# Memory's matrices woven with the first gated units, and the last pair's sum on VectorE, in a hybrid encoder layer

## The chip, the cores and the metric

The kernel runs on one core of a Trainium2 chip. The metric is the device time of one execution in microseconds. The core has five engines that run side by side: TensorE (PE in the profile, with its weight loads as PEld), VectorE (DVE), ScalarE (ACT), GpSimd (POOL) and SyncE (SP), whose queue issues most DMA transfers; ScalarE's queue issues a few.

## The reference, cut to what matters

One layer of an encoder on 2048 tokens of width 1024, batch 1, all in float32:

```python
y = rmsnorm(h, norm_mix_g) @ w_in            # q, k, v (8 heads of 64), a and g (512 each)
att = dilated_sliding_attention(q, k, v)     # three patterns (window, dilation), joined by a softmax of their log-sums
conv = silu(layernorm(conv31(a * sigmoid(g)) + conv_b))
h = h + concat([att, conv]) @ w_out
xq = rmsnorm(h) @ w_xq
xk, xv = rmsnorm(mem) @ w_xk, rmsnorm(mem) @ w_xv      # mem: 256 rows
h = h + softmax(xq @ xk.T / 16) @ xv @ w_xo            # 4 heads of 256
h = h + square(relu(rmsnorm(h) @ w_up)) @ w_down       # 4096 wide
out = rmsnorm(h, norm_final_g)
```

Everything that depends on `mem` is known before any token is read, so the kernel multiplies it together once: w_xq with xk (the matrices "a", `ascr`) and xv with w_xo (the matrices "b", `bscr`). These are "memory's matrices". The three patterns of attention give three partial results with their minima and sums; a "pair" is two neighbouring heads, and "the pair's sum" joins its three partial results.

## The kernel before, in words

**Precision.** Each matmul operand is split in a high half (rounded to fp32r) and a low half (the rest). A product takes three matmuls, high by high, high by low, low by high (`mm3`, L197 to L200). A weight tile is loaded as `raw` (128 x 1024, 512 KB), its high half is a cast on ScalarE, its low half a subtraction on VectorE or POOL (`wsplit2`, L186; `split` in `memory`, L380).

**The planner.** The program is traced in an order written out by hand: generators that yield, and `weave` (L92), which takes one step of a main generator and then, by a rate, steps of the others; `run` (L455) does the same with whole numbers of steps. A scheduler then goes through the traced instructions by priority in the order of the trace, on a simulated time line, and gives each engine and each DMA queue its order: what stands earlier in the trace goes first, and what is ready in the simulation fills the gaps. `pinned` and `after` (L78 to L90) hold an instruction behind a given one on its engine. On the chip each engine and each queue keeps that order strictly. A tile waits until the last tile in its place (same pool and tag) has been read for the last time; PSUM tiles share eight banks by kind (`banks`, L65).

**First stage (L710 to L727).** Token group n (of four, 512 tokens each) has a room `x{n}` of eight tiles for its high and low halves of normalized x. `memory` (L346) makes memory's matrices: after two first steps eight steps for w_xk (`proj`), twelve for w_xq (`xq`, transposed; four heads, two tiles each), eight for w_xv, twelve for w_xo (four heads, two tiles each). It borrows the room of group 3 for its activations and, for its weights, two places in the weight pool and two in the room of group 2 (`wtiles`, L371): four raw tiles, four high and four low halves in turn. `xprep(n)` (L320) loads 512 rows of x, takes their norms and, in eight steps, transposes 128 columns of all four blocks on PE, copies the transpose out (`xts`, L334, to the scratch `xscr`), scales it (`xv`, L337) and splits it (L338 ScalarE, L339 POOL). The order is `run([memory, xprep 0 and 1], (3, 1))`, then the gated units `glu(0)` and `glu(1)` on groups 0 and 1 (`glu`, L490: g through a sigmoid, a times that), of which one step and then seven are woven with `xprep` 2 and 3 at a rate of 2.5. Then `edges` (L700) writes zero rows from a tile in a raw weight place, and `lin_qk` (L589) projects keys and queries with their rotary part (`ct`, `sn`, L634 to L645) on all four groups.

**Values and the first convolution (L737 to L747).** `lin_v` projects v; the depthwise convolution of group 0 (`conv0`, 31 steps of 128x512 on VectorE per channel block, L213 and L215) is woven into it, in the last part at a rate of 1.2.

**Attention on group 0 (L1080 to L1110).** The far pattern is done for all tokens here. The gated units on groups 2 and 3 (`rest`) run ahead for 32 steps and then at 0.8 of a step per step of attention; the layernorm of the convolution (`conv_ln`, L221) stands first in the weave. A unit of attention has scores (`s`), masked minimum and exponential (L762, L763), transposes (L769), probabilities in two halves (L772, L773) and products with v (L777 to L779).

**A pair's sum (`combine`, L871).** It loads two partial results (`ld`), takes the minimum on VectorE (L890, L891), and then, on engine `W`, which is POOL: differences (L892, L894), after an exponential on ScalarE (L898) the weighted sums (L900 to L905), after a reciprocal on VectorE (L909) the weights (L912) and the weighted parts (L916, L918). The result `cat` is transposed on PE (L926), split (`ct`, L928, L929), stored to the scratch `cath` and `catl`, and loaded again for the output projection by `load_cat` and `load_pair` (L1154 to L1170). For group 0, `load_pair` for the last two pairs is called late, inside `resid_linear` (L1172), ahead of the last third of the first three output tiles.

**After that (`post`, L1197)** come, for each group, the output projection, cross attention, and the wide layer, woven with the attention and the convolution of the next group; the first six steps of `post(0)` are woven with the end of attention on group 0.

Of the kernel before, what the change touches and what calls it, by code (L numbers as in the profile page):

```python
# [21 lines left out]
P = 128  # L22
S = 2048
D = 1024
H = 8
# [22 lines left out]
def hybrid_layer(ctx, tc, A, out):  # L48
# [16 lines left out]
    banks = {"mm": (0, 1, 2), "a": (3, 4), "b": (5, 6), "c": (7,), "mem": "b"}  # L65
# [254 lines left out]
    def xprep(sp, n):  # L320
# [8 lines left out]
        for k in range(KC):  # L329
            pt = ps("a", f"xt{n}_{k}")  # L330
            for j in range(4):
                PE.transpose(pt[:, j * P:(j + 1) * P], nat_cols(nat[j], k), ident)
# [4 lines left out]
            DVE.scalar_tensor_tensor(xv, pt, gain("mix", k), rbs, op0=ALU.mult, op1=ALU.mult)  # L337
            ACT.copy(XH_[k, n], xv)  # L338
            POOL.tensor_tensor(XL_[k, n], xv, f(XH_[k, n]), op=ALU.subtract)  # L339
            yield  # L340
# [5 lines left out]
    def memory(sp):  # L346
# [24 lines left out]
        def wtiles(name, shape=(P, 8, P)):  # L371
            i = cnt[0] % 4
            cnt[0] += 1
            if i < 2:
                return [wp.tile(list(shape), dt, tag=t, name=f"m{t}_{name}", bufs=2)
                        for t, dt in (("raw", F32), ("whi", F32R), ("wlo", F32R))]
            return [xpool(q, j, 2, f"m{q}{j}_{name}", shape, dt)
                    for q, j, dt in (("h", i - 2, F32), ("h", i, F32R), ("l", i, F32R))]

        def split(src, name, shape=(P, 8, P)):  # L380
            raw, hi, lo = wtiles(name, shape)
            dma(raw, src)
            ACT.copy(hi, raw)
            DVE.tensor_tensor(lo, raw, f(hi), op=ALU.subtract)
            return hi, lo

        def proj(w, name, th, tl):

            for j in range(KC):
                wh, wl = split(wcols(w, j * P), f"{name}{j}")  # L390
                pt = ps("mm", f"p{name}{j}")[:, 0:256]
# [13 lines left out]
        for h in range(XH):  # L405
# [15 lines left out]
            for k2 in range(4):  # L421
                pt = ps("mm", f"pa{h}{k2}")
# [12 lines left out]
        for h in range(XH):  # L435
# [4 lines left out]
            for mc in range(2):  # L440
                for nh in range(2):
                    pt = ps("mm", f"pb{h}{mc}{nh}")
# [11 lines left out]

    def run(gens, steps):  # L455

        live = list(zip(gens, steps))
        while live:
            for g in list(live):
                for _ in range(g[1]):  # L460
                    if next(g[0], live) is live:
                        live.remove(g)
                        break
# [246 lines left out]
    with ExitStack() as st:  # L710
# [26 lines left out]
    with ExitStack() as st:  # L737
# [8 lines left out]
        weave(steps, (conv0, 1.2))  # L746
# [123 lines left out]

    def combine(p, pr, o0):  # L871
# [15 lines left out]
        W = POOL  # L887
# [33 lines left out]
        ct = [aq.tile([P, 512], F32R, tag=f"ct{x}", name=f"ct{x}{p}{pr}") for x in "hl"]  # L921
# [8 lines left out]
        for t, d in zip(ct, (cath, catl)):  # L930
            dma(f(d[pr][:, 512 * p:512 * (p + 1)]), f(t))
# [150 lines left out]
    with ExitStack() as st:  # L1082
# [5 lines left out]
        for _ in range(32):  # L1088
# [63 lines left out]
    cats = {}  # L1152

    def load_cat(p, half):  # L1154
# [17 lines left out]
    def resid_linear(load, rhs, korder, resid, hs, ssum, key, y, name, late=None):  # L1172


        for ms in ((0, 1, 2), (3,), (4,), (5,), (6,), (7,)):
            wt = [load(m) for m in ms]
            pts = {}
            for i, ks in enumerate((korder[0:4], korder[4:6], korder[6:8]) if len(ms) > 1 else (korder,)):
                if late and len(ms) > 1 and i == 2:
                    late()  # L1180
                for m, (wh, wl) in zip(ms, wt):
# [4 lines left out]
                    if late and ks[-1] != korder[-1]:  # L1186
# [10 lines left out]
    def post(p):  # L1197
# [9 lines left out]
        def from_x(m):  # L1207
# [8 lines left out]
                                (lambda: load_pair(0, 1, 1)) if p == 0 else None)  # L1216
# [195 lines left out]
```

## Time and profile before

| | us |
|---|---|
| median of 3 runs | 2928.93 (2924.41 to 2935.4) |
| the profiled execution's own time | 2929.9 |
| its span, first to last instruction | 2928.1 |
| PE busy in it | 2845.6 |

The profile is of one execution. Busy time of an engine is the time covered by its instructions; a row of a group gives the line, engine, operation and tiles, the count, then busy us and mean ns of one, and the idle time ahead of them with what ended it. A row of the timeline gives the start in us from the span's start, the duration, the instruction, and in brackets how long its engine had been idle and what released it. A row of a stretch gives its length and each engine's busy time in it, the mean clock that TensorE was granted (1 is full speed) and the share of the DMA engines' time.

### The profile page before, as it was taken

To read this page: it belongs to the slowest core of one execution; us is meant where nothing else is said; L and a number is where in the kernel's file an instruction comes from. 1 tells how busy PE (TensorE), PEld (TensorE's weight loads), DVE (VectorE), ACT (ScalarE), POOL (GpSimd) and SP (SyncE) were. 2 spreads that over 40 slices of the span, in tenths; PEclk is the share of its full clock that TensorE was granted. 3 is DMA by queue.
4 is the path that set the end of the run, shared out by engine and by line. 5 is a ranking of instruction groups with operands and counts; after the bars stand their busy time and mean duration, and the time that the engine had idled before them with its cause. 6 is when DMAs were issued, how large, how long until landed. Compare 5 with 4: busy or idle time off the path is not lost.

```text
span 2928.1 us, 42935 instructions
## 1 busy us (share of the span) xinstructions
PE 2845.6 (97%) x16396; PEld 2426.2 (83%) x16396; DVE 1845.9 (63%) x3295; ACT 1186.9 (41%) x2002; POOL 462.9 (16%) x518
## 2 busy tenths in 40 slices
PE   8999999989799999999999999999999999999999
PEld 7878789878698888888888888888888888888887
DVE  5636544555568877566697865577877555544445
ACT  5632211566435333444443344344433443432233
POOL 1335421122101220210020122000210110000000
PEclk9999999999899999999999999999999999999999
DMA  8978854799724444455344445534444355333332
GB/s 263 304 161 205 194 146 135 172 239 230 206 93 133 129 134 136 138 167 172 97 128 129 136 130 177 181 101 131 121 132 132 113 153 173 94 93 94 96 99 73
DMA packets 620806, 434.89 MB, mean 149 GB/s; under 512 B 191333, under 2 KB 549785, under 8 KB 620600
## 3 DMA queue, kind: packets, MB, share of 16 engines
q1 hardware_dynamic: 582168, 414.05, 50.3%
q10 hardware_dynamic: 38432, 18.09, 2.6%
q8 instruction: 129, 2.11, 0.3%
q14 instruction: 77, 0.63, 0.1%
HBM read 340.42 MB, written 91.64 MB: 148 GB/s over the span
## 4 chain that ended last, share of the span: by engine, by line
PE 75%; DMA 4%; ACT 2%; DVE 2%; SPq 2%; issue 1%; POOL 1%; ACTq 0%; POOLq 0%; DVEq 0%
PE dn L198 8%; PE dn L199 8%; PE dn L200 8%; PE up L198 8%; PE up L200 8%; PE up L199 7%; PE xs L198 2%; PE xs L199 2%; PE xs L200 2%; PE o L198 2%; PE o L199 2%; SPq L57 2%; PE o L200 2%; PE pt L769 2%; PE s L979 2%; PE x L198 2%
## 5 line engine op out<-in xcount | busy, mean ns | idle before, releaser
L198 PE MATMUL up<-mh,whi_u 128*128 128x512 f32 x1024 | 402.9, 394 | 1.3 <-DVE rl L1283 1.1
L199 PE MATMUL dn<-hhl,whi_d 128*128 128x512 f32 (+1 forms) x1056 | 402.5, 385 | 0.4 <-DVE hhl L1286 0.4
L200 PE MATMUL dn<-hhh,wlo_d 128*128 128x512 f32 (+1 forms) x1056 | 401.6, 384 | 0.0
L198 PE MATMUL dn<-hhh,whi_d 128*128 128x512 f32 (+1 forms) x1056 | 400.3, 391 | 0.1
L200 PE MATMUL up<-mh,wlo_u 128*128 128x512 f32 x1024 | 399.4, 390 | 0.0
L199 PE MATMUL up<-ml,whi_u 128*128 128x512 f32 x1024 | 398.6, 389 | 0.0
L215 DVE SCALAR_TENSOR_TENSOR cacc<-cu,cw,cacc 128x512 f32<-128x512 f32 x480 | 387.7, 808 | 5.8
L189 ACT CAST whi_u<-raw_u 128x1024 fp32r<-128x1024 f32 x128 | 134.6, 1052 | 428.2 <-PE dn L199 358.5
L1301 DVE TENSOR_TENSOR h<-h,dn 128x512 f32<-128x512 f32 (+1 forms) x264 | 172.5, 668 | 203.3 <-PE dn L200 202.3
L189 ACT CAST whi_d<-raw_d 128x1024 fp32r<-128x1024 f32 x128 | 134.4, 1050 | 355.4 <-PE up L199 318.3
L200 PEld LDWEIGHTS dn<-hhh,wlo_d 128*128 128x128 f32 x1056 | 198.5, 188 | 39.3
L198 PEld LDWEIGHTS dn<-hhh,whi_d 128*128 128x128 f32 x1056 | 197.5, 188 | 39.3 <-DVE h L1301 3.5
L199 PEld LDWEIGHTS dn<-hhl,whi_d 128*128 128x128 f32 x1056 | 198.8, 188 | 36.4 <-DVE hhl L1286 1.0
L200 PEld LDWEIGHTS up<-mh,wlo_u 128*128 128x128 f32 x1024 | 192.2, 188 | 40.8
L198 PEld LDWEIGHTS up<-mh,whi_u 128*128 128x128 f32 x1024 | 192.1, 188 | 39.9 <-DVE rl L1283 1.8
L199 PEld LDWEIGHTS up<-ml,whi_u 128*128 128x128 f32 x1024 | 192.4, 188 | 38.1
L1283 DVE SCALAR_TENSOR_TENSOR rl<-up,ssumx 128x512 f32<-128x512 f32 x128 | 87.9, 690 | 201.3 <-PE up L200 196.5
L763 ACT ACTIVATE sm<-sm,o 128x256 f32<-128x256 f32 (+1 forms) x384 | 158.9, 465 | 115.3 <-DVE o L762 103.2
L190 DVE TENSOR_TENSOR wlo_u<-raw_u,whi_u 128x1024 fp32r<-128x1024 f32 x128 | 163.5, 1277 | 28.0 <-ACT whi_u L189 27.4
L190 DVE TENSOR_TENSOR wlo_d<-raw_d,whi_d 128x1024 fp32r<-128x1024 f32 x128 | 159.0, 1242 | 28.6 <-ACT whi_d L189 28.6
L762 DVE CUSTOM_DVE_ANT_0 sm<-s,mask 128x256 f32<-128x256 f32 (+1 forms) x384 | 127.8, 375 | 54.1 <-PE s L979 34.3
L198 PE MATMUL xs<-whi_a,yh 128*128 128x256 f32 x512 | 146.7, 289 | 1.3 <-DVE o L762 1.3
(390 smaller groups left out, 6498.4 us busy)
## 6 DMA issues: line engine op xcount, KB each, us to landing
raw_u<-in_w_up_dram SPq DMA_DIRECT2D x128, 512.0 KB
raw_d<-in_w_down_dram SPq DMA_DIRECT2D x128, 512.0 KB
raw_o<-in_w_out_dram SPq DMA_DIRECT2D x32, 512.0 KB
raw_a<-ascr SPq DMA_DIRECT2D x32, 512.0 KB
raw_b<-bscr SPq DMA_DIRECT2D x32, 512.0 KB
v<-vtok SPq DMA_DIRECT2D x208, 65.0 KB
k<-kscr SPq DMA_DIRECT2D x24, 512.0 KB
k<-kscr SPq DMA_DIRECT2D x8, 1152.0 KB
```

The costliest lines, as they stand in the source:

```text
L57: (q or nc.sync).dma_start(o, i)
L189: ACT.copy(hi, raw)
L190: (lo_eng or DVE).tensor_tensor(lo, raw, f(hi), op=ALU.subtract)
L198: PE.matmul(o, lh, rh, start=first, stop=False)
L199: PE.matmul(o, lh, rl, start=False, stop=False)
L200: last["pe"] = PE.matmul(o, ll, rh, start=False, stop=end)
L215: DVE.scalar_tensor_tensor(acc, u[:, t:t + 512], cw[:, c, t:t + 1], acc, op0=ALU.mult, op1=ALU.add)
L762: last["dve"] = DVE.tensor_tensor_reduce(dst, so, mask[:, 256 * m:256 * m + nk], 1.0, 3e38, ALU.add, ALU.min, mn)
L763: last["act"] = ACT.activation(dst, dst, AF.Exp, bias=mn, scale=-1.0)
L769: last["pe"] = PE.transpose(pt[:, j, :], sm[:, j, :], ident)
L1283: last["dve"] = DVE.scalar_tensor_tensor(r, pt, 0.0, rsb, op0=ALU.max, op1=ALU.mult)
L1301: last["dve"] = DVE.tensor_tensor(hs[m][:, sl], hs[m][:, sl], pt, op=ALU.add)
```

## The change

- **Memory's weights** no longer use the weight pool. Their raw tiles turn through four places in the room of group 2 (`h0`, `h1`, `l0`, `l1`), their high and low halves through two (`h2`, `h3` and `l2`, `l3`). Every second low half of `split` is subtracted on POOL.
- **Order of the first stage.** Memory's next 15 steps are woven with `xprep` 0 and 1 at 1.25. Then the remaining ones are the main order, with `glu(0)` in fine steps (three matmuls each) beside them at 1.35, 32 steps. Then four steps of `glu(1)` are woven with `xprep` 2 and 3 at 4.5. The gated units use PSUM banks 3 and 4 while memory lasts, memory 0 to 2 (kind `m`). `run` goes.
- **`xprep`**: every second copy out of PSUM is on ScalarE.
- **`conv0`** goes at 2.2 in its last part; `rest` runs ahead for 38 steps and then at 0.75.
- **The last pair's sum on group 0** (`end`) has VectorE as `W`; its two halves go straight into the tiles that the output projection reads, with no store and no load. The loads of the pair before it move into `load_cat`, and the late call goes.

```diff
@@ xprep
-            DVE.tensor_copy(xt, pt)
+            (ACT.copy if k % 2 else DVE.tensor_copy)(xt, pt)
@@ memory
         def wtiles(name, shape=(P, 8, P)):
-            i = cnt[0] % 4
+            i = cnt[0]
             cnt[0] += 1
-            if i < 2:
-                return [wp.tile(list(shape), dt, tag=t, name=f"m{t}_{name}", bufs=2)
-                        for t, dt in (("raw", F32), ("whi", F32R), ("wlo", F32R))]
             return [xpool(q, j, 2, f"m{q}{j}_{name}", shape, dt)
-                    for q, j, dt in (("h", i - 2, F32), ("h", i, F32R), ("l", i, F32R))]
+                    for q, j, dt in (("hl"[i % 4 // 2], i % 2, F32), ("h", 2 + i % 2, F32R), ("l", 2 + i % 2, F32R))]
         def split(src, name, shape=(P, 8, P)):
+            lo_eng = POOL if cnt[0] % 2 else DVE
...
-            DVE.tensor_tensor(lo, raw, f(hi), op=ALU.subtract)
+            lo_eng.tensor_tensor(lo, raw, f(hi), op=ALU.subtract)
@@ the first stage
-        run([mg, chain(xprep(sp, 0), xprep(sp, 1))], (3, 1))
+        first = chain(xprep(sp, 0), xprep(sp, 1))
+        weave(islice(mg, 15), (first, 1.25))
+        drain(first)
+        banks["mm"] = (3, 4)
         alln = tuple(range(NG))
-        banks["mm"] = (0, 1, 2, 5, 6)
         early01 = (0, 1)
-        units = list(chain(glu(0, early01), glu(1, early01)))
+        units = list(chain(glu(0, early01, True), glu(1, early01)))
...
-        next(steps)
+        weave(mg, (islice(steps, 32), 1.35))
+        banks["mm"] = (0, 1, 2, 5, 6)
         later = chain(xprep(sp, 2), xprep(sp, 3))
-        weave(islice(steps, 7), (later, 2.5))
+        weave(islice(steps, 4), (later, 4.5))
         drain(later)
@@ lin_v
-        weave(steps, (conv0, 1.2))
+        weave(steps, (conv0, 2.2))
@@ combine
-        W = POOL
+        end = p == 0 and pr == H // 2 - 1
+        W = DVE if end else POOL
...
-        ct = [aq.tile([P, 512], F32R, tag=f"ct{x}", name=f"ct{x}{p}{pr}") for x in "hl"]
+        ct = [cats[0][x, pr] if end else aq.tile([P, 512], F32R, tag=f"ct{x}", name=f"ct{x}{p}{pr}") for x in "hl"]
...
-        for t, d in zip(ct, (cath, catl)):
+        for t, d in () if end else zip(ct, (cath, catl)):
             dma(f(d[pr][:, 512 * p:512 * (p + 1)]), f(t))
@@ attention on group 0
-        for _ in range(32):
+        for _ in range(38):
             next(rest)
...
-        weave(islice(first, 50), (ln0, 0.33), (rest, 0.8))
+        weave(islice(first, 50), (ln0, 0.33), (rest, 0.75))
...
-        weave(islice(first, 74), (rest, 0.8))
+        weave(islice(first, 74), (rest, 0.75))
@@ load_cat, load_pair, resid_linear
-            if j == 0 or half == 0 or p:
-                load_pair(p, half, j)
+            load_pair(p, half, j)
...
-            for e in range(2):
+            for e in range(1 if p == 0 and half and j else 2):
...
-                if late and len(ms) > 1 and i == 2:
-                    late()
```

Elsewhere `"mm"` becomes `"m"` in `memory`, and the flag `late` of `resid_linear` a flag `steps`.

More of the change, by code (lines that the diff above doesn't have):

```diff
@@ L63, in hybrid_layer @@
     psp = pool("psp", PSUM)
-    banks = {"mm": (0, 1, 2), "a": (3, 4), "b": (5, 6), "c": (7,), "mem": "b"}
+    banks = {"m": (0, 1, 2), "a": (3, 4), "b": (5, 6), "c": (7,), "mem": "b"}
     turn = {}
@@ L390, in proj @@
                 wh, wl = split(wcols(w, j * P), f"{name}{j}")
-                pt = ps("mm", f"p{name}{j}")[:, 0:256]
+                pt = ps("m", f"p{name}{j}")[:, 0:256]
                 for k in range(KC):
@@ L453, in memory @@
             yield
[L455 to L463, printed above, removed]
     def linear(wh, wl, n):
@@ L1185, in resid_linear @@
                         mm3(pts[m], wh[:, k, :], wl[:, k, :], rhs["h", k], rhs["l", k], k == korder[0], k == korder[-1])
-                    if late and ks[-1] != korder[-1]:
+                    if steps and ks[-1] != korder[-1]:
                         yield
```

12 lines of the change are left out of this document (6 added, 6 removed).

## The prediction

> **What bounds the kernel now.** Three views, in this order: the page's engine shares, the busy time by stretch, and the waits and the timeline inside the stretches that stand out.
>
> ```profile
> span 2928.1 us, 42935 instructions
> PE 2845.6 (97%) x16396; PEld 2426.2 (83%) x16396; DVE 1845.9 (63%) x3295; ACT 1186.9 (41%) x2002; POOL 462.9 (16%) x518
> ```
>
> PE is the bound, with 2928.1 - 2845.6 = 82.5 us idle. The change moves matmuls and takes none away, so it can win only PE's idle time and its time at a reduced clock. Where these are:
>
> ```profile
> core 0: us, PE busy (x) PEld busy (x) DVE busy (x) ACT busy (x) POOL busy (x), PEclk, DMA share, GB/s
> 0.00:20.00 20.00, 10.66 (x47) 8.49 (x48) 7.40 (x20) 11.28 (x24) 1.40 (x7) 0.94 0.74 208
> 20.00:90.00 70.00, 64.25 (x511) 61.92 (x511) 51.74 (x88) 43.44 (x95) 20.71 (x15) 0.97 0.97 295
> 90.00:141.00 51.00, 50.34 (x321) 45.04 (x320) 33.00 (x44) 35.21 (x62) 15.85 (x10) 1.00 0.94 292
> 190.00:212.00 22.00, 15.36 (x67) 12.40 (x66) 6.59 (x10) 5.25 (x10) 10.67 (x10) 0.84 0.82 221
> ...
> 538.00:546.00 8.00, 4.35 (x22) 3.62 (x21) 2.65 (x18) 4.20 (x10) 2.36 (x1) 0.84 0.91 227
> ...
> 766.00:790.00 24.00, 8.24 (x50) 6.02 (x49) 8.70 (x20) 4.04 (x9) 10.63 (x18) 0.63 0.72 189
> ...
> L200 PE MATMUL pb<-mh_xo,tlv x16: 389/389/398, 118.9 to 141.0; 128*128 128x512 f32 x16
> ...
> L339 POOL TENSOR_TENSOR xl<-xv,xh x32: 1280/1294/2357, 38.2 to 211.9; 128x512 fp32r<-128x512 f32 x32
> ```
>
> Read the second number (PE busy) against the first, and PEclk; the last two rows are of the views of two tiles, with the shortest, median and longest duration in ns and the first and last start. The last of memory's matmuls starts at 141, the last piece of x at 212; the stretches are cut there, where attention on the first tokens begins (538) and where the output projection takes over from it (790). Idle: 9.3 in the start, 5.8 in 20 to 90, 0.7 in 90 to 141, 6.6 in 190 to 212, 3.7 in 538 to 546, 15.8 in 766 to 790. A clock of 0.97 over 70 us costs 2.1 more, 0.84 over 22 us 3.5. From 20 to 141 the DMA engines are as full as PE (0.97 and 0.94). The change reaches all of these places.
>
> **Part 1: memory and the first gated units.** Before, memory's weight tiles lie partly in the weight pool, so the gated units wait for memory's end. After, glu 0 on two token groups (96 matmuls of 512 columns) stands between memory's last 24 steps, and the first two preparations of x (72 transposes) between the 15 ahead of them. Each keeps its cost:
>
> ```profile
> 191.39 0.60 PE L332 MATMUL xt<-ident,xn 128*128 128x128 f32 x4
> ...
> 210.95 0.39 PE L198 MATMUL lin<-xh,whi_kr 128*128 128x512 f32 x1
> 211.18 0.39 PE L199 MATMUL lin<-xl,whi_kr 128*128 128x512 f32 x1
> ```
>
> Starts are 0.23 us apart, so the gated work is 96 x 0.23 = 22 us; four transposes take 0.60, a single one at least 0.27, so (0.60 - 0.27) / 3 = 0.11 apiece and 8 us for 72. These 30 us are cover for waits inside memory. What memory pays: four pairs of high and low halves become two. A head of w_xq or of w_xo fills both, so the next head's halves are made only after this head's last matmul. Twelve of 24 low halves go from VectorE to POOL, and 16 of 32 copies of x from VectorE to ScalarE.
>
> ```profile
> L384 DVE TENSOR_TENSOR mwlo_xo<-mraw_xo,mwhi_xo 128x1024 fp32r<-128x1024 f32 x4 | 4.9, 1220 | 1.2 <-ACT mwhi_xo L383 1.2
> L384 DVE TENSOR_TENSOR mwlo_xv<-mraw_xv,mwhi_xv 128x1024 fp32r<-128x1024 f32 x4 | 6.4, 1611 | 0.2 <-ACT mwhi_xv L383 0.2
> L383 ACT CAST mwhi_xo<-mraw_xo 128x1024 fp32r<-128x1024 f32 x4 | 4.2, 1042 | 0.8 <-PE pxv L199 0.8
> L190 POOL TENSOR_TENSOR wlo_g<-raw_g,whi_g 128x1024 fp32r<-128x1024 f32 x2 | 4.8, 2396 | 6.2 <-ACT whi_g L189 6.2
> L417 DVE TENSOR_TENSOR ml_xq<-xqt,mh_xq 128x512 fp32r<-128x512 f32 x8 | 5.3, 684 | 0.2 <-ACT mh_xq L416 0.2
> L416 ACT CAST mh_xq<-xqt 128x512 fp32r<-128x512 f32 x8 | 4.6, 584 | 4.0 <-PE xqt L414 3.9
> L327 ACT COPY rbs<-rb 128x512 f32<-128x512 f32 x3 | 1.8, 586 | 1.6 <-PE rb L184 1.6
> ```
>
> Between two heads of w_xo, uncovered: two casts (2.08) and a POOL low half (2.40), less the three matmuls (0.7) that the first tile allows: 3.8 us, three times 11.4. Between two of w_xq: a cast (0.58) and three low halves (2.05), with handovers 3 us, three times 9. For w_xk and w_xv, 1.04 + 2.40 for a POOL tile stands against 26 matmuls of 256 columns, 3.0 us at half of 0.23 each: 0.4, eight times 3.5. Together 24 us, with 30 of cover in the same stretch, so I count them as covered. The ScalarE copies cost 16 x 0.59 = 9.4 us on an engine that idles 26.6 of 70 there: nothing; were that cover gone, up to 9.4. All transfers stay, and x's 8 MB of loads and stores move ahead of w_xk and w_xq on the SP queue, in a stretch whose DMA engines are already full: so the idle 5.8, the 2.1 of clock and the 0.7 don't all go. Bounds: 8.6 won, 24 lost. I take **3 us won**, near the upper end, since cover exceeds price.
>
> The Trainium skill ("SBUF — State Buffer", section "Who interferes with whom") says that a VectorE instruction with two SBUF inputs and a GpSimd instruction that reads SBUF exclude each other for the whole instruction. The trace agrees: the same subtraction took 1611 ns for w_xv against 1220 for w_xo. It speaks against low halves on POOL, and makes a rival below.
>
> **Part 2: the later preparations of x.** The 6.6 us at 197 to 205:
>
> ```profile
> 168.29 0.38 SPq L57 DMA_DIRECT2D xn<-in_x_dram  x1
> ...
> 179.48 1.34 SPq L57 DMA_DIRECT2D vtok<-zrow  x2
> ...
> 192.55 1.92 SPq L57 DMA_DIRECT2D raw_k<-in_w_in_dram  x3
> 194.51 0.70 SPq L57 DMA_DIRECT2D ct_kr<-in_rope_dram  x1
> ...
> 199.49 0.69 DVE L643 TENSOR_TENSOR ct_kr<-lin,ct_kr 128x512 f32<-128x512 f32 x1 [9.82 <-DMA ct_kr<-in_rope_dram]
> ...
> 204.57 1.08 PE L332 MATMUL xt<-ident,xn 128*128 128x128 f32 x4 [6.64 <-DVE xv L337]
> ```
>
> On the SP queue, raw_k waits for the weight buffer that the zero rows still hold; ct_kr, behind it, comes late; VectorE stands 9.8 us at L643, and x's last pieces queue behind L643. PE waits for them. After, 18 steps of x go into four gated steps, not seven, so these pieces should be ahead of L643. Against it: the cover. From memory's end to x's took 212 - 141 = 71 us; now PE has only glu 1 (22 us), 8 us of transposes and two units of kr (48 x 0.23 = 11), 41 in all. Bounds: 6.6 + 3.5 = 10.1 won; lost, should the 71 us stay, 71 - 41 = 30 idle against 10.1 now, 20. I take **7 won**, two thirds of what is idle or slow there: what is late is VectorE's order, and the change mends that order.
>
> **Part 3: the seam into attention.** conv0's rate goes from 1.2 to 2.2, and 38 steps of the gated rest, not 32, stand ahead of attention.
>
> ```profile
> 517.28 5.47 DVE L215 SCALAR_TENSOR_TENSOR cacc<-cu,cw,cacc 128x512 f32<-128x512 f32 x7
> 522.78 0.32 SPq L57 DMA_DIRECT2D cscr<-cacc  x1
> 535.44 0.58 SPq L57 DMA_DIRECT2D lc<-cscr  x1
> 541.91 0.69 DVE L240 TENSOR_TENSOR lsum<-lsum,lc 128x512 f32<-128x512 f32 x1 [3.30 <-DMA lc<-cscr]
> ```
>
> The convolution's last part ends at 522.8, its reload is issued at 535.4, and VectorE stands 3.3 us at L240 with attention's first softmax behind it. With its last ten steps spread over 5 steps of v rather than 8, the store comes before attention, and that wait goes. Six steps of three matmuls put 6 x 0.69 = 4.1 us of work ahead of attention, where 3.7 are idle, and take them out from under attention. Bounds: 5 won (3.7 idle, 1.3 of clock), 4.1 lost if attention misses them. **3 won.** The faster convolution queues the v evictions behind it; five PSUM banks cover that, and without them PE would wait a few us.
>
> **Part 4: the last pair's sum.**
>
> ```profile
> 769.37 0.17 DVE L891 TENSOR_TENSOR csm<-csm,o 128x8 f32<-128x8 f32 x1
> 770.18 0.22 ACT L898 ACTIVATE ce<-ce 128x24 f32<-128x24 f32 x1 [2.27 <-POOL ce L894]
> ...
> 775.84 0.21 PE L777 MATMUL opt<-v,ph 128*128 128x65 f16 x1 [6.75 <-DMA v<-vtok]
> 777.86 0.24 PE L779 MATMUL opt<-v,pl 128*128 128x65 f16 x1
> 780.03 1.07 POOL L810 CAST ql<-ql 64x512 fp32r<-64x512 f32 x1
> 781.07 1.17 POOL L918 TENSOR_TENSOR cat<-cat,ld 128x512 f32<-128x512 f32 x1
> 782.29 1.11 PE L926 MATMUL catT<-ident,cat 128*128 128x128 f32 x4 [4.19 <-POOL cat L918]
> 784.16 0.75 DVE L929 SCALAR_TENSOR_TENSOR ctl<-catT,vinv,cth 128x512 fp32r<-128x512 f32 x1 [6.85 <-ACT cth L928]
> 789.10 1.65 PE L198 MATMUL o<-cath,whi_o 128*128 128x512 f32 x3 [0.88 <-DMA cath<-cath]
> ```
>
> From L891's end (769.54) POOL needs until 782.24. On VectorE: 12 small operations like L891 (12 x 0.17 = 2.0), the exponential (L898, 0.22) for which I take 0.8 with the way there and back, and five of 128x512 at 0.69 (L240 is such an operation) = 3.5; in sum 6.3, done at 775.8. PE gets its v at the same time (775.84) and finishes the products on it at 778.1. So the next late thing is v, and catT starts at about 778.1, not 782.29: 4.2 won. L929 ends 2.6 after catT starts, at 780.7. Before, 784.91 to 789.10 went to the store and the reload of both parts; kept on chip, these 4.2 us go, but some 2 us of attention's matmuls that ran under them must now stand somewhere. 4.2 + 4.2 - 2 = 6.4, rounded to **6 won** for convolution operations of 0.75 that may slip between. Bounds: 15.8 (all idle) and, should VectorE be held up throughout, 2.2. The two loads of pair 2 move up to the first load on the SP queue; a planner that puts them before their store holds what is behind for about 2 us: none counted.
>
> **Sum.** 3 + 7 + 3 + 6 = 19. The profiled run took 2929.9 us, its span is 2928.1, the median of three runs is 2928.93: 2929.9 - 19 = 2910.9, and 1 less on the median's scale, **2910**. Under about 0.5% (14.6 us), a difference can't be told from none here.
>
> **The rivals.**
> - Only the seams gain (parts 3 and 4, 9 us): memory is bound by its transfers (0.97 of the DMA share speaks for it), and the planner had already put gated units under it as far as it could. **2920**, chance 0.15.
> - Slower: x's chain keeps its 71 us. It is bound by buffers and the queue, not by the spacing on PE, and PE stands in it with 41 us of cover: 20 lost in part 2, part 1 worth nothing, parts 3 and 4 won: 2929 + 20 - 9 = **2940**. It decides as soon as the chain exceeds 41 us by more than the other parts win. For it: a load of x came as late as 168; against it: it waited for transposes that stood behind gated units, of which there are now fewer. Chance 0.13.
> - All of it: parts 1 to 4 reach 8 + 10 + 4 + 11 = 33: **2896**. For it: all idle places named here have their own cover. Chance 0.14.
> - VectorE and POOL in each other's way: each of the 12 POOL low halves holds up one subtraction by 1611 - 1220 = 0.39 us, 5 in all, and the two casts between POOL's last sums (1.07 each) hold VectorE's sum by 2: 19 - 7 = 12 won, **2917**. For it: xl's longest is 2357 against a median of 1294; against it: both can work beside PE in part 1. Chance 0.06. (The rule of the Trainium skill told in part 1 would have it so.)
> - The change does not do what it says (the planner keeps the old order): within these, as the part it concerns falls to nothing.
>
> **How the numbers follow.** The forecast has 0.52, with its own range of 2900 to 2920. Range 2894 to 2940: it reaches to the full gain and to the slow chain, and leaves about a tenth out at each end. Faster by over 0.5% means below 2914.3: some seven tenths of the forecast (0.36), the full gain (0.14), a third of the seams' case and of VectorE's and POOL's (0.07): **0.57**. Slower means above 2943.6: under half of the slow chain (0.05) and what I haven't thought of (0.04): **0.09**. The rest, **0.34**, is within.
>
> **What would show it.** Part 1: gated matmuls before 140 and PE idle under 4 us from 20 to memory's end; wrong if PE's waits name w_xq's or w_xo's low halves for over 10 us. Part 2: no wait of xt for xv over 2 us; wrong if PE's wait for x's pieces grows. Part 3: L240 no longer waits for its reload. Part 4: L916 and L918 of the last pair on VectorE, their end no more than 8 us after L891's, no wait for cath's reload, and catT right behind the products on v; wrong if PE still starts the projection's last part some 20 us after L891. Any stall after 800 that wasn't there would fall outside all this.

## The result, and the profile after

| | before | after |
|---|---|---|
| median of six runs each (us) | 2927.64 (2924.41 to 2935.40) | 2948.55 (2946.02 to 2952.69) |
| profiled execution (us) | 2929.9, span 2928.1 | 2948.32, span 2946.4 |
| ratio after to before | | 1.0069, 95% interval 1.0054 to 1.0084 |

The change makes the kernel 20 us slower, where 19 us faster was forecast. The page of after:

```profile
span 2946.4 us, 42942 instructions
PE 2857.3 (97%) x16396; PEld 2431.0 (83%) x16396; DVE 1821.2 (62%) x3283; ACT 1194.1 (41%) x2018; POOL 479.6 (16%) x514
```

PE carries out the same 16396 matmuls. The span is 18.3 us longer, but idle time (span less busy) grew only from 82.5 to 89.1, by 6.6. The other 11.7 us stand in busy PE: matmuls that took longer. So the loss can't be read from idle time alone: the number of matmuls in a stretch and the granted clock are needed too. The busy time by stretch, first after, then the rows of before for the same stretches that the prediction has not shown:

```profile
core 0: us, PE busy (x) PEld busy (x) DVE busy (x) ACT busy (x) POOL busy (x), PEclk, DMA share, GB/s
20.00:90.00 70.00, 60.83 (x461) 57.15 (x460) 42.09 (x73) 45.56 (x97) 32.77 (x21) 0.95 1.01 302
90.00:141.00 51.00, 51.00 (x334) 46.76 (x334) 13.88 (x25) 21.47 (x34) 16.82 (x9) 1.00 0.60 169
141.00:180.00 39.00, 35.59 (x150) 25.93 (x150) 7.06 (x9) 16.83 (x25) 11.90 (x6) 1.00 0.70 192
180.00:212.00 32.00, 25.61 (x117) 21.18 (x116) 12.27 (x16) 13.50 (x24) 9.00 (x8) 0.91 0.78 160
250.00:300.00 50.00, 38.65 (x151) 30.32 (x150) 29.52 (x32) 16.32 (x23) 35.54 (x27) 0.90 0.90 212
515.00:546.00 31.00, 31.00 (x224) 29.35 (x222) 18.15 (x30) 3.58 (x9) 2.15 (x5) 1.00 0.63 184
```

```profile
141.00:180.00 39.00, 39.00 (x183) 32.34 (x182) 9.06 (x18) 12.28 (x19) 10.91 (x7) 1.00 0.64 141
180.00:212.00 32.00, 25.36 (x115) 20.76 (x115) 13.32 (x19) 9.59 (x15) 14.06 (x12) 0.89 0.84 187
250.00:300.00 50.00, 50.00 (x224) 41.46 (x223) 40.27 (x47) 15.21 (x24) 31.06 (x27) 1.00 0.90 213
```

Three places got worse. From 20 to 90, idle is 9.2 against 5.8 and the clock 0.95 against 0.97. From 141 to 180 there are 3.4 idle where there were none. From 250 to 300, PE was full before, with 224 matmuls of the projections; after it did 151 of the same shape. The 73 that are missing are 73 x 0.23 = 17 us: 11.4 idle and the rest a clock of 0.90. The gap at 180 to 212, which part 2 was to close, stands as it was: 6.4 idle against 6.6. How far behind after is, the last starts of memory's matmuls (pb), of x's pieces (xl) and of v tell; the first three rows are of after, the fourth of before:

```profile
L200 PE MATMUL pb<-mh_xo,tlv x32: 387/393/402, 143.3 to 174.1; 128*128 128x512 f32 x32
L339 POOL TENSOR_TENSOR xl<-xv,xh x32: 1270/1288/1869, 32.2 to 248.0; 128x512 fp32r<-128x512 f32 x32
L200 PE MATMUL v<-wvh,xl x256: 278/284/284, 423.0 to 536.3; 128*128 128x256 f32 x128
```

```profile
L200 PE MATMUL v<-wvh,xl x256: 283/283/415, 400.6 to 515.3; 128*128 128x256 f32 x128
```

At the end of v, after is 21 us behind. At the end of the kernel it is 18.3 behind, so all of the loss was made ahead of attention. Memory's last matmul comes 33 us later than before (174.1 against 141.0), though only 22 us of gated work were put under it. And x's last piece comes 248.0 - 174.1 = 74 us behind memory's last matmul, where it came 212 - 141 = 71 us behind it before. PE's waits in after, from 20 to 320 (total, times, longest):

```profile
PE xt L332 <- DVE xv L337: 8.0, 3, 6.4
PE lin L198 <- DVE ct_qr L631: 6.9, 2, 6.2
PE pxk L200 <- DVE ml_xk L382: 2.7, 3, 1.7
PE pb L199 <- POOL ml_xo L382: 1.7, 2, 1.4
```

The old wait for x's pieces (6.4, at 207) is still there, and a new one has come: at 272.75 PE waits 6.2 us for a PSUM bank that VectorE frees only when the rotation's table for q has been loaded and multiplied (L631). The convolution's last sum still waits for its reload (2.6 us at L240, at 540), which part 3 said would be gone; no softmax stands behind it on VectorE there, as the next instruction does not come before 553. The last pair's sum, by contrast, did what it should. VectorE's and PE's rows of after:

```profile
796.28 0.17 DVE L885 TENSOR_TENSOR csm<-csm,o 128x8 f32<-128x8 f32 x1
...
802.88 0.68 DVE L912 TENSOR_TENSOR cat<-cat,ld 128x512 f32<-128x512 f32 x1
```

```profile
803.62 1.12 PE L920 MATMUL catT<-ident,cat 128*128 128x128 f32 x4
805.51 1.65 PE L198 MATMUL o<-cath,whi_o 128*128 128x512 f32 x3 [0.78 <-ACT cath L922]
```

From the end of L885 (796.45) to the projection's restart (805.51) there are 9.1 us; before, from 769.54 to 789.10, 19.6.

### The profile page after: what moved, and what is told of

Read it like the earlier page. It is cut to its first block, busy times and chain, and to the rows that moved or that the text cites. A ratio compares the mean times of both kernels' runs of the same rounds, so it can differ in the third digit from the quotient of the medians.

```text
span 2946.4 us, 42942 instructions
## 1 busy us (share of the span) xinstructions
PE 2857.3 (97%) x16396; PEld 2431.0 (83%) x16396; DVE 1821.2 (62%) x3283; ACT 1194.1 (41%) x2018; POOL 479.6 (16%) x514
## 4 chain that ended last, share of the span: by engine, by line
PE 84%; DMA 3%; ACT 2%; DVE 2%; issue 2%; POOL 1%; SPq 1%; ACTq 0%; POOLq 0%; DVEq 0%
PE dn L198 8%; PE dn L199 8%; PE dn L200 8%; PE up L198 7%; PE up L200 7%; PE up L199 7%; PE lin L198 3%; PE lin L199 3%; PE lin L200 3%; PE xs L198 2%; PE xs L199 2%; PE xs L200 2%; PE x L198 2%; PE o L198 2%; PE s L973 2%; PE o L199 2%
```

## The experiments

The theory after this reading (A): x's later preparations need some 70 us from memory's end, PE has too little else to do beside them once the first gated unit has been used up under memory, and what follows them is late with them. The rival (B): memory itself pays for its new room, by two pairs of halves in place of four, by low halves on POOL, or by x's loads ahead of its weights. Each ratio is to runs of before on the same chip, with the 95% interval; the medians of before were 2928.8 to 2936.2 on these chips, so 0.001 is 2.9 us.

### Which parts lose

**Parts 3 and 4 alone** (the first stage as before):

```diff
-        weave(steps, (conv0, 1.2))
+        weave(steps, (conv0, 2.2))
@@ combine, load_cat, load_pair, resid_linear: as in the change
@@ attention on group 0: 38 and 0.75, as in the change
```

> The first stage as before, only parts 3 and 4 (the seam into attention, the last pair's sum). As forecast these two win 9 us: 2927.6 - 9 = 2919. The trace of after says less: between the first and the last piece of the last pair's sum and the projection's last part it won 10 us, but attention ahead of it lost some 6: 2924. If the loss of after comes from these two parts, this kernel is slower than before, 2930 or more.

Measured: 1.0001 (0.9990 to 1.0011). Neither the forecast's 9 us won nor a loss.

**Part 4 alone** (the edits of combine, load_cat, load_pair and resid_linear):

> Part 4 alone (the last pair's sum on VectorE, kept on chip). Forecast: 6 won, 2922. The trace of after would allow 10: 2918. If part 3 costs what attention lost in after, this kernel beats the one with both parts by some 6 us; if part 3 wins its 3, it is 3 us behind it.

Measured: 0.9990 (0.9982 to 0.9999), 3 us won. Its trace stood some 7 us behind that of before at 740, ahead of anything that the edit touches, so the kernel before was profiled once more:

> The kernel before, unchanged, for its trace on the chip that runs the next three: the kernel with the sum alone had the orders of before up to the last sum, and yet its trace stood 7 us later at 740. If that is the chip, this trace shows the same 7 between 546 and 740; if it is the sum's edit, this trace stands where that of before stood.

Measured: 2933.02 in one run, and at 740 it stood within a microsecond of the first trace of before. By what was put down, that lays the 7 us on the edit. But this control ran on chip 3 and the sum alone on chip 8, so it does not rule the chip out; and up to the last sum the engines of the sum's kernel have the orders of before. The busy time in attention, first of this control, then of the sum alone:

```profile
546.00:766.00 220.00, 200.61 (x1741) 173.09 (x1739) 123.84 (x495) 145.65 (x319) 39.60 (x59) 0.95 0.91 219
```

```profile
546.00:766.00 220.00, 201.01 (x1717) 174.07 (x1716) 122.87 (x498) 142.60 (x312) 39.59 (x59) 0.94 0.90 216
```

PE is as busy with 24 matmuls fewer, at a lower granted clock: the same work took longer in this execution. Whether the edit has a part in that, the traces don't show. The seam itself is to be read from the sum's first row on. The two rows of the control, then the two of the sum alone:

```profile
771.32 0.17 DVE L891 TENSOR_TENSOR csm<-csm,o 128x8 f32<-128x8 f32 x1
```

```profile
790.52 1.65 PE L198 MATMUL o<-cath,whi_o 128*128 128x512 f32 x3 [0.83 <-DMA cath<-cath]
```

```profile
776.75 0.17 DVE L894 TENSOR_TENSOR csm<-csm,o 128x8 f32<-128x8 f32 x1
```

```profile
789.55 1.65 PE L198 MATMUL o<-cath,whi_o 128*128 128x512 f32 x3 [0.78 <-ACT cath L931]
```

That is 790.52 - 771.49 = 19.0 against 789.55 - 776.92 = 12.6: 6.4 us won in place, of which the times show 3 (0.3 to 5.3). Most of it is the store and reload that are gone. The sum itself ended only here:

```profile
785.89 1.71 DVE L921 TENSOR_TENSOR cat<-cat,ld 128x512 f32<-128x512 f32 x2
```

That is 787.60, 10.7 us behind its second row, where POOL's took 12.2 in the control: convolution operations and attention's own ones stood between its parts on VectorE. In after it took 803.56 - 796.45 = 7.1.

**Parts 1 and 2 alone** (the first stage of after; both seams as before):

> Parts 1 and 2 alone (memory, the first gated units, x's later preparations); both seams as before. If the early stage is the whole loss, and the parts add up: the milestone at the end of v stood 21 us later in after, so 2927.6 + 21 = 2949 or a little above after. If the parts are not additive (the loss of after lies in what the seams do), 2928 or below.

Measured: 1.0073 (1.0061 to 1.0085). The first stage is the whole loss.

### What the first stage pays

**The cover given back.** After, with the first gated unit behind memory:

```diff
-        units = list(chain(glu(0, early01, True), glu(1, early01)))
+        units = list(chain(glu(0, early01), glu(1, early01)))
...
-        weave(mg, (islice(steps, 32), 1.35))
+        drain(mg)
...
-        weave(islice(steps, 4), (later, 4.5))
+        next(steps)
+        weave(islice(steps, 7), (later, 2.5))
```

> After, but the first gated unit isn't woven with memory: it stands behind it, with seven gated steps of 24 matmuls for the two later preparations of x, as before. Theory A (x's later preparations need some 70 us beside PE work and have 41): their cover is back, the waits at 200 to 290 go, memory loses the cover of 22 us but keeps what x gives it: about 2928, at most 2935. Theory B (memory pays for its own halved rings and for x's loads ahead of its weights): the waits stay inside memory and grow when the gated matmuls are gone: 2945 to 2965.

Measured: 1.0038 (1.0024 to 1.0051): 2942.8 against 2934.9. About half of the loss went, and half stayed: A and B both have a part. From 250 to 300 PE was full again.

**Half of it given back**:

```diff
-        weave(mg, (islice(steps, 32), 1.35))
+        weave(mg, (islice(steps, 16), 0.7))
...
-        weave(islice(steps, 4), (later, 4.5))
+        weave(islice(steps, 16), (later, 0.9))
+        weave(islice(steps, 4), (later, 0.9))
```

> After, with only the first half of the first gated unit (48 of 96 matmuls, 11 us) under memory, the other half and the second unit as cover of x's later preparations. With the whole unit behind memory 1.0038, with none of it 1.0069. If the loss follows the cover: 1.0045 to 1.006. If the chain needs no more than it then has (52 us), 1.003 to 1.0045 and no wait of PE for the rope's product in 250 to 290; if it needs all, 1.0065.

Measured: 1.0020 (1.0011 to 1.0029). Its stretch from 250 to 300:

```profile
250.00:300.00 50.00, 47.12 (x201) 38.12 (x199) 35.55 (x40) 14.43 (x26) 31.22 (x25) 0.97 0.96 233
```

Of the 73 missing matmuls 50 are back. The loss does not follow the cover in proportion: the second half of the unit cost 0.0049 (14 us) when it went under memory, and the first half cost nothing that can be seen (1.0020 against 1.0038 for none; the intervals overlap a little). The point from which it loses lies between 52 and 41 us of PE work beside x's chain. The edit also spreads x's steps evenly, so this is a point for the two together. What sets the length of x's chain is not shown: here it took 65 us (169.0 to 234.1), and PE's longest wait in it was 7.6 us for a load of x.

**SP's queue.** In after, the stores of x's late pieces stand ahead of the rotation's loads in SP's order. They were put on ScalarE's queue:

```diff
-            dma(xscr[k][:, 512 * n:512 * (n + 1)], xt)
+            dma(xscr[k][:, 512 * n:512 * (n + 1)], xt, nc.scalar if n > 1 else None)
```

> After, with the stores of x's two later preparations issued on ScalarE's queue in place of SP's. Theory A1 (what is late in 250 to 290 is SP's order: the rope's loads stand behind x's stores): PE's wait for the first product with the rope goes, some 6 to 16 us won against after, ratio to before about 1.003. Theory A2 (x's chain itself is long, and PE has too little else to do): the waits stay, ratio 1.006 to 1.008.

Measured: 1.0056 (1.0041 to 1.0071), not to be told from after. But the experiment did not free the queue, as its trace shows. SP's waits from 215 to 270, in after and in this kernel, and this kernel's queue:

```profile
SPq L57 <- DVE xts L334: 19.4, 4, 8.6
```

```profile
SPq L57 <- DVE xv L337: 18.4, 1, 18.4
```

```profile
224.72 21.13 SPq L57 DMA_DIRECT2D cu<-uscr  x2
245.96 0.39 SPq L57 DMA_DIRECT2D ct_qr<-in_rope_dram  x1
```

With x's stores gone, the convolution's load of cu stands in their place: it goes into the room that x's preparation uses up to its last piece, and waits for it. So the rotation's table for q comes at 246.0, against 247.4 in after: behind x's chain in either case. What that does to the rotation's product for q (durations, first and last start), in before and in after:

```profile
L643 DVE TENSOR_TENSOR ct_qr<-lin,ct_qr x4: 671/684/692, 228.9 to 262.2; 128x512 f32<-128x512 f32 x4
```

```profile
L631 DVE TENSOR_TENSOR ct_qr<-lin,ct_qr x4: 677/684/691, 254.7 to 291.5; 128x512 f32<-128x512 f32 x4
```

The four products lie 11 to 12 us apart in both, on a chain over ScalarE, POOL, VectorE and loads, though PE needs 24 x 0.23 = 5.5 us for each. In before that chain began at 228.9 and had other projections beside it. In after PE ran q's first matmuls from 219 on, while x's last pieces were still being made; their product came at 254.7, 26 us later than in before, and the banks were held. So A1's queue is in it, but not by the stores alone, and an order of SP that lets the table past both was not tried.

**x's loads ahead of memory's weights.** The kernel with the whole cover given back, and x at one step per three of memory's:

```diff
-        weave(islice(mg, 15), (first, 1.25))
-        drain(first)
...
-        drain(mg)
+        weave(mg, (first, 0.334))
+        drain(first)
```

> The kernel with the cover given back (first gated unit behind memory), and x's first two preparations at one step per three of memory's, as before, in place of 1.25 steps per step. What is left of part 1 is memory's own: two pairs of halves in place of four, low halves on POOL, copies on ScalarE. That kernel lost about 9 us more than before ahead of 141. Theory B1 (x's loads ahead of memory's weights cost it): they come back, ratio 0.998 to 1.001. Theory B2 (the halved rings and POOL's low halves cost it): they stay, ratio 1.003 or more.

Measured: 1.0025 (1.0013 to 1.0038), against 1.0038 (1.0024 to 1.0051) with x ahead: most of it stays, and a share of x's order can't be told.

**The engines alone**, on before with its four pairs of halves (every second low half on POOL, every second copy of x on ScalarE):

> Before, with the two changes of engine alone: every second low half of memory's weights on POOL, every second copy of x on ScalarE; four pairs of halves, x and the gated units as before. If POOL's low halves are what memory pays (with slower x, SP waited 11.9 us for them), a good part of the 7 us that stayed there shows here: ratio 1.001 to 1.003. If the halved rings are what it pays, no difference, 0.999 to 1.001.

Measured: 0.9996 (0.9983 to 1.0009).

**The rings alone** (the kernel with slower x, all low halves and copies on VectorE):

> The other half: memory's weights in two pairs of halves outside the weight pool, with all low halves and copies on VectorE as before, the first gated unit behind memory and x one step per three; both seams as in after. If the rings are what memory pays, ratio 1.002 to 1.004; if POOL's low halves are, 0.999 to 1.001.

Measured: 1.0006 (0.9995 to 1.0018). So neither costs anything that the times show by itself, while both together came to 1.0025; the intervals of 1.0025 and 1.0006 overlap by a little. In place the traces show more. Memory's last matmuls, with both, and with the rings alone:

```profile
L200 PE MATMUL pb<-mh_xo,tlv x32: 387/396/402, 126.5 to 157.4; 128*128 128x512 f32 x32
```

```profile
L200 PE MATMUL pb<-mh_xo,tlv x32: 387/393/402, 125.1 to 152.4; 128*128 128x512 f32 x32
```

Before, the last one started at 141.0, behind about as many matmuls (876, against 885 in both kernels here), and in the nine other executions with memory as before at 140.5 to 143.3. So with the rings alone memory ends 11 us later, and with POOL's low halves and ScalarE's copies 5 more; at the end of v the rings alone are 5 us behind before, and both 9 (515.3, 520.3, 524.7). The times, 2 and 7 us more than before, fit that within their intervals. What SP waited for in 20 to 160, with both, and with the rings alone:

```profile
SPq L57 <- POOL ml_xv L382: 11.9, 4, 5.2
...
SPq L57 <- POOL ml_xo L382: 7.0, 2, 4.9
```

```profile
SPq L57 <- DVE tlv L395: 15.4, 6, 3.5
...
SPq L57 <- DVE ea L428: 9.1, 9, 2.9
```

With both, SP stands 18.9 us behind low halves on POOL, which take 2.39 us each where VectorE takes 1.22. But all its waits in this stretch come to 74 us with both and to 71 with the rings alone, so the queue as a whole hardly waits longer. PE itself waits 4.3 us for the low halves of w_xv and w_xo with both (3.8 of them for POOL's), and 1.6 with the rings alone. What makes the rest of the 5 us is open.

**POOL's low halves in after itself** (lo_eng = DVE throughout):

> After, with all low halves of memory's weights on VectorE. With x slower and the first gated unit behind memory, the same edit won some 5 us. If POOL holds up memory's two pairs of halves here too: after's 1.0069 less 0.002, 1.005. If the gated matmuls under memory hide it: 1.0065 to 1.007.

Measured: 1.0058 (1.0042 to 1.0075): 0.001 less than after, as B would have it, but well within the intervals. In the trace memory's last matmul starts 6 us earlier than in after (168.0 against 174.1) and v ends 4 us earlier (532.0 against 536.3). Open.

### What the right edits are worth

**Part 2's spacing with its full cover**, on before:

```diff
-        weave(islice(steps, 7), (later, 2.5))
+        weave(islice(steps, 4), (later, 4.5))
         drain(later)
+        for _ in range(3):
+            next(steps)
```

> Before, with part 2's spacing alone: x's two later preparations in four of the eight gated steps at 4.5, not in seven at 2.5, and the last gated steps behind them. Their cover is as before (44 us of gated work and the transposes). If the spacing is right and only the cover was missing in after, PE's wait at 197 to 205 goes and this is up to 7 us faster than before (ratio 0.9976). If the chain is bound by its buffers and its queue whatever the spacing, no difference, or PE waits for x inside the gated steps (ratio 1.000 to 1.003).

Measured: 0.9987 (0.9977 to 0.9996), 4 us won. The stretch of the old wait and the one behind it, first in the control, then here, and x's last pieces here:

```profile
180.00:212.00 32.00, 25.09 (x114) 20.36 (x113) 13.41 (x20) 9.11 (x14) 13.47 (x11) 0.89 0.81 181
...
250.00:300.00 50.00, 50.00 (x223) 41.13 (x222) 40.07 (x48) 15.18 (x24) 31.09 (x26) 1.00 0.91 220
```

```profile
180.00:212.00 32.00, 32.00 (x151) 26.52 (x150) 14.56 (x20) 9.37 (x13) 11.62 (x13) 1.00 0.82 179
...
250.00:300.00 50.00, 46.43 (x199) 37.61 (x198) 41.07 (x49) 15.14 (x24) 31.70 (x28) 0.97 0.92 224
```

```profile
L339 POOL TENSOR_TENSOR xl<-xv,xh x32: 1277/1294/2353, 37.9 to 202.3; 128x512 fp32r<-128x512 f32 x32
```

The wait at 197 to 205 is gone and x's chain is 10 us shorter. From 250 to 300, however, 24 matmuls are missing, 5.5 us (PE waits 2.2 for the eviction of k and 1.3 for the rotation's product): that much of the gain is given back there. At the end of v this trace is where the control's is (515.0 against 514.2), so the traces do not show where the 4 us of the times are won.

**The two right edits together** (spacing and sum):

> The two edits that looked right alone, together on before: x's spacing inside its full cover (4 won alone) and the last pair's sum on VectorE (3 won alone); memory and the seam into attention as before. Additive: 7 won, ratio 0.9975. If the wins of one are taken up by attention's own chain, 0.9987 to 0.999.

Measured: 0.9986 (0.9977 to 0.9995): not additive, but the interval takes in 0.998.

**The same and the convolution's rate of 2.2**:

> The same and the convolution's rate of 2.2, without the six gated steps moved ahead of attention. If part 3 lost because the moved steps are missing under attention, the faster convolution alone keeps its wait of 3.3 to 4.2 at L240 and this kernel is 3 to 4 us faster than the one without it. If attention's start isn't what sets its end, no difference.

Measured: 0.9944 (0.9932 to 0.9957): 2921.3 against 2936.0, and 12 us better than without the rate, three times what was expected. The convolution's last sum, without the rate and with it:

```profile
543.94 0.69 DVE L240 TENSOR_TENSOR lsum<-lsum,lc 128x512 f32<-128x512 f32 x1 [5.02 <-DMA lc<-cscr]
```

```profile
521.12 0.69 DVE L240 TENSOR_TENSOR lsum<-lsum,lc 128x512 f32<-128x512 f32 x1 [3.12 <-DMA lc<-cscr]
```

It still waits for its reload, but 23 us earlier, where no softmax stands behind it. PE's stretch from 515 to 546, without and with:

```profile
515.00:546.00 31.00, 25.63 (x123) 21.54 (x122) 12.25 (x29) 6.66 (x12) 6.67 (x4) 0.97 0.77 186
```

```profile
515.00:546.00 31.00, 31.00 (x172) 26.45 (x171) 6.99 (x32) 8.84 (x19) 6.63 (x4) 1.00 0.85 217
```

**The six gated steps moved ahead of attention**, added to that kernel (38 and 0.75):

> The best kernel so far (spacing, sum, faster convolution: 0.9944) with the six gated steps moved ahead of attention (38 in place of 32, then 0.75 per step). If these steps are needed as cover under attention, the 10 to 12 us that the convolution won are gone again: ratio 0.997 to 0.9995. If the convolution had won only because of the spacing and the sum, no loss: 0.9944.

Measured: 1.0002 (0.9991 to 1.0013): all of it gone. Its waits of PE in the first 200 us of attention (515 to 746), first without the moved steps, then with them:

```profile
PE opt L779 <- ACT ph L774: 5.5, 5, 2.5
PE pt L771 <- ACT sm L765: 3.8, 6, 1.6
PE opt L781 <- DVE pl L775: 3.4, 8, 0.5
```

```profile
PE pt L771 <- ACT sm L765: 8.9, 8, 2.4
PE opt L781 <- DVE pl L775: 8.5, 15, 1.0
PE opt L779 <- ACT ph L774: 4.7, 6, 2.1
```

12.7 us of waits for attention's own softmax became 22.1: the gated steps had been PE's work under these waits. The traces show 9 us of it. The two profiles' whole times differ by only 4 us, since that of the moved kernel was its shortest run, 2924.1 against a median of 2928.8, and had reached the end of v 8 us earlier than the other (509.0 against 516.8).

**Six steps fewer ahead of attention** (26 and 0.85):

> The same kernel with six gated steps fewer ahead of attention (26, then 0.85 per step). If every step that runs under attention instead of ahead of it is won, 4 us more: 0.993. If attention has all the cover that it can use at 32, no difference or some us lost, since PE then waits for the chain at attention's start: 0.9944 to 0.996.

Measured: 0.9973 (0.9959 to 0.9988). Not better than 32, if anything some us worse; against the repeat of 32 below (0.9940 to 0.9967) the intervals overlap.

**After, mended** (half of the first unit under memory, low halves on VectorE, 32 and 0.8), and **the best kernel again**, on one chip:

> After, mended in three places that the runs named: half of the first gated unit under memory (1.0020), low halves all on VectorE (0.001 won in after), and the gated rest at 32 steps and 0.8 as before (up to 0.006 won). If these add up: 1.0020 - 0.001 - 0.005 = 0.996. If it stays behind the next kernel, the new room for memory's matrices is worth nothing even without its three costs.

> The best kernel so far once more (memory as before; spacing, sum, faster convolution), on the same chip as the one above: 0.9944 the first time. With 0.993 to 0.996 its gain stands; the one nearer to 0.999 than that would say that the first call had met a chip on which it is faster than usual.

Measured: 0.9980 (0.9971 to 0.9989), and 0.9953 (0.9940 to 0.9967): 2927.6 and 2919.5 against 2933.6. The best version leaves memory as it was, and takes from the change the spacing of x, the sum on VectorE and the convolution's rate. The mended one comes 8 us behind it: without the three costs that were taken out, what is left of part 1 (the new room, x's loads ahead, half of the gated unit under memory, copies on ScalarE) still wins nothing over memory as it was.

## Why the prediction was wrong

Nested kernels give an account. The ratios are each to before on its own chip, and the differences add up to 1.0069 by construction; most of them carry more than one edit. The best kernel has 0.9953. Memory's new room and what goes with it instead of the old adds 0.0027; POOL's low halves and the six moved steps 0.0040; the second half of the first unit under memory, with x's closer spacing, 0.0049: that is after. In us: 14 won by what is right, 8, 12 and 14 lost.

- **Part 1 failed at the step "30 of cover in the same stretch, so I count them as covered".** The cover was not free: the first unit's 22 us were already the cover of x's later preparations, and a matmul covers once. The step weighed price and cover inside memory's stretch alone. Giving half of that cover back, with x's steps spread evenly, took the ratio from 1.0069 to 1.0020. The price of 24 us was real too, if too high: with no gated work under it, memory ended 16 us later than before, 11 of them with the two pairs of halves alone. It did not come where the prediction looked for it: in after, PE's waits for w_xq's and w_xo's halves came to 4 us (0.8, 1.3, 1.7 and 0.4), not to over 10, and those for w_xk's to 2.9; PE's idle time from 20 to 180 was 12.6, where under 4 had been expected. In the times, rings and POOL alone each cost nothing that could be measured; both together, with the copies on ScalarE, 0.0019 (6 us) more than the rings, by intervals that overlap. How that is paid is open.
- **Part 2 failed at "what is late is VectorE's order, and the change mends that order".** The order was half of it: the same spacing with the whole cover won 4 us of the forecast's 7. The prediction had the other half as a rival, "x's chain keeps its 71 us" (it took 74), with 41 us of cover, and gave it 0.13, since fewer gated units stand before the transposes. With the whole cover and the closer spacing the chain took 61 us (65 with after's memory and the old spacing), with 41 us of cover 74: it gets no shorter for having fewer gated units in its way. The rival's 20 us of loss in the stage came out at 21 (end of v), but that nearness is in part luck: the rival had memory itself at nothing, and about half of the loss stayed when the whole cover was given back. The place was another one too. PE's long wait for x's pieces stayed as it was (6.4 us against 6.6); PE spent the rotation's projections as cover and then stood at 250 to 300.
- **Part 3's "3 won" was a sum of two terms of opposite sign, both mis-sized.** The convolution's rate, on top of the spacing and the sum, won 12 us (10 by the repeat), where the prediction saw a wait of 3.3 in it; the six moved steps cost 14 to 17 (the bound was 4.1, "if attention misses them"; it does). A step under attention covers more than its own 0.69 us: the traces show 9 us more of waits for six steps of 4.1 us. What made the rest of the 14 is open.
- **Part 4 was right in mechanism, and near in size**: kept on chip and without the reload, the way from the sum's second row to the projection got 6.4 us shorter alone and 10.5 in after, where 4.2 + 4.2 had been counted in place. In after the sum ended 7.1 us behind L885 (8 allowed), no wait for a reload was left, and catT began at once. Alone it ended 10.7 behind, over what was allowed, so 1.5 of the 6.4 came from the sum and 4.9 from the store and reload. The times show 3 us; the 6 of the forecast lie just outside their interval (0.3 to 5.3).
- **VectorE and POOL in each other's way** had 0.06. The Trainium skill ("SBUF — State Buffer", section "Who interferes with whom") has such instructions exclude each other. The traces agree at single instructions. In the kernel with the two changes of engine alone:

```profile
105.62 2.27 DVE L385 TENSOR_TENSOR mwlo_xo<-mraw_xo,mwhi_xo 128x1024 fp32r<-128x1024 f32 x1 [0.58 <-ACT mwhi_xo L384]
```

A subtraction on POOL ran from 104.39 to 106.80 beside it; undisturbed, this one takes 1.22. Six of VectorE's twelve there took 1.38 to 2.27, each beside an instruction on POOL, 3.5 us more in all, where the rival had 5. But they did not stand where they cost time: the whole kernel came to 0.9996 (0.9983 to 1.0009).

The range's upper end, 2940, was the slow chain with parts 3 and 4 won. It missed that three things could come at once: the slow chain, a price inside memory, and no gain at the seams.

## What to carry to other kernels

Before work is moved as cover to a new place, list what it covers where it is: a filler that leaves one chain's shadow opens that chain, and the wait may show up two stages later, as missing matmuls and a lower clock more than as idle time. Two edits that each cost nothing in the times may cost together, when one lengthens the step that the other makes scarce (a slower engine and fewer buffers); here that is likely, not shown. A change of several parts is best forecast and tested by its parts, since here a gain of 14 us was hidden behind losses of 34.

## What the runs showed of the hardware

- More than half of the loss was no idle time: of 18.3 us of span 11.7 lie in longer busy PE. In after's stretches with the larger gaps (20 to 90, 180 to 212, 250 to 300) the granted clock was 0.90 to 0.95; from 141 to 180, with 3.4 idle in small pieces, it stayed at 1.00.
- A load that needs room which another chain still uses holds up all that stands behind it on SP: cu's held the rotation's table for 21 us in one kernel.
- A subtraction of 128x1024 on VectorE takes 1.22 us alone and up to 2.27 beside one on POOL in the kernel with the two changes of engine, whose time is nevertheless that of before (0.9996).
- Attention with the same orders of instructions took 5 us more in one profiled execution than in another, with 24 matmuls fewer in the same busy time. Two executions of the best kernel on two chips, with the same orders on every engine, reached the end of v 4 us apart (516.8 and 513.0). So a difference of 5 us between two traces is no finding by itself; the ratios of many runs are.
